# Rope's last two steps from GpSimd to VectorE, and the causal convolution's multiply-adds spread earlier, in a two-layer decoder trunk

## The chip, the core and the metric

The kernel runs on one core of a Trainium2 chip. A core has TensorE (matrix products and transposes, PE in the profile), VectorE (DVE), ScalarE (ACT), GpSimd (POOL) and SyncE (SP, which here only issues DMAs). The metric is the device time of one execution in microseconds; the kernel before takes 2527.41 us (median of three runs, 2525.86 to 2529.16).

## The reference, cut to what matters

Each of two layers does: a half-step SwiGLU feed-forward block, a mixer of three parallel branches, and another half-step feed-forward block. All data are float32, 512 positions by 1024 features. The change lies in the mixer:

```
qa, ka, va, qc, kc, vc, conv_in, gate_pre = split(h @ w_in)
rope(x)  = [x1*cos - x2*sin, x2*cos + x1*sin]        # on qa, ka, qc, kc; head size 64
oa = dilated_attention(rope(qa), rope(ka), va)       # 3 groups of 4 heads
z  = a * sigmoid(gt)                                 # a, gt = halves of conv_in, 512 channels
y[t] = sum_j w[j] * z[t - 30 + j] + b                # causal depthwise convolution, 31 taps
ob = silu(layernorm(y))                              # over the 512 channels
oc = differential_attention(rope(qc), rope(kc), vc)
x += postnorm((g0*proj_a(oa) + g1*proj_b(ob) + g2*proj_c(oc)) @ w_out)   # g = sigmoid gates
```

## The kernel before, in words

**Products.** Every float32 operand of a large product is split into a high part (`hi`, rounded by ScalarE, line 120) and a low part (`lo`, the difference, by VectorE, line 121); a product is then three matmuls (`mm3`, lines 138 to 140). `split` does this for a weight chunk of 128 columns. Four pairs of `hi` and `lo` buffers (`HLB`) let the splits run ahead of TensorE. The weights come through two 1 MB `raw` buffers, loaded by SyncE.

**Order of the work.** The program is one straight line; a planner places the instructions on each engine's queue by priority (earlier in the program first) among those that its own cost model takes to be ready. On the chip each queue is then worked off in that order, waits included.

**The mixer's order** (line 434 on): the first conv projection `conv(0)` (two of four channel tiles), eight differential q and k chunks with rope (`turned(0)`, `turned(1)`, which call `rotate`; `heads` after each), the differential value projection `vc`, the differential attention, twelve dilated q and k chunks with rope (`rope`; the first two of `qa` and of `ka` are plain, the other eight `phased`, written in strided order), the value projections `va0` and `va1`, the second conv projection `conv(2)`, dilated attention, and the gates and output projections (lines 760 to 809). Projections use three PSUM banks with the tag `pm`, and one `ps`.

**Rope** (`rotate`, lines 516 to 531). The projection lies in a PSUM bank. ScalarE copies it to `raw` (line 519), VectorE multiplies the bank by the cosine into the destination (line 526; the bank is free once both have read it), four DMAs issued by ScalarE's queue move the 32-row halves to `sw` (line 529), GpSimd multiplies `sw` by the sine (line 530) and adds it to the destination (line 531).

**The convolution.** The 31 taps of a channel tile are 31 VectorE instructions on `y` (lines 496 and 498), four tiles a layer, 124 in all. `conv_taps(rate)` puts the taps of the finished `z` tiles in a list, `tapq`, and sets `pace`; each later `split` takes up to `pace` taps off the list, and each tap gets an ordering edge behind that split's `lo`. In the kernel before, `conv_taps(2)` stands behind `vc` and the second `heads`, and `conv_taps(3)` behind the first dilated attention group. What is left at the end of the gates is put behind the last branch product (`flush`, lines 774 and 775). Then comes the convolution's layer norm: transposes of `y` (line 781), statistics, and transposes back (line 793).

Of the kernel before, what the change touches and what calls it, by code (L numbers as in the profile page):

```python
# [49 lines left out]
def kernel(ctx: ExitStack, tc: tile.TileContext, a, out):  # L50
    nc = tc.nc
    V, S, G, PE, SY = nc.vector, nc.scalar, nc.gpsimd, nc.tensor, nc.sync
# [10 lines left out]
    def bank(tag, shape=(P, T)):  # L63
        return psum.tile(list(shape), F32, tag=tag, name=tag, bufs=BANKS[tag])
# [47 lines left out]
    pace = [0]  # L112
# [18 lines left out]
    def col_chunks(src, c0, c1, step=256):  # L131
        for c in range(c0, c1, step):
            raw = load(src[:, c:c + step], KD, step)
            for s in range(0, step, P):
                yield c + s, split(raw[:, :, s:s + P])
# [6 lines left out]
    def proj_group(chunks, hh, hl):  # L142
        ps = [bank("pm") for _ in chunks]
        for p_, (wh, wl) in zip(ps, chunks):
            for k in range(KD):
                mm3(p_, wh[:, k, :], wl[:, k, :], hh[:, k, :], hl[:, k, :], k == 0, k == KD - 1)
        return ps
# [27 lines left out]
    def proj_lead(w, c0, c1, hh, hl, spare, raws=None):  # L175
        if raws is None:
            raws = [load(w[j][:, c:c + 256], KD, 256) for j, c in ((0, c0), (1, c1))]
        wts = {}
        for f in range(2):
            for j in range(2):  # L180
                raw = raws[j][:, :, f * P:(f + 1) * P]
                if (f, j) != (1, 1):
                    wh, wl = split(raw)
                    wts[f, j] = [(wh[:, k, :], wl[:, k, :]) for k in range(KD)]
                else:
                    wts[f, j] = []
                    for s in range(0, KD, 4):
                        pair_ = [z.rearrange("p (k n) -> p k n", n=P) for z in spare()]
                        wh, wl = split(raw[:, s:s + 4, :], pair_)
                        wts[f, j] += [(wh[:, k, :], wl[:, k, :]) for k in range(4)]  # L190
        H = T // 2
        whole = [bank("pm") for _ in range(2)]
        parts = []
        for s in range(2):
            c = slice(s * H, (s + 1) * H)
            two = bank(("pm", "po")[s])
            parts.append(two)
            outs = [whole[0][:, c], whole[1][:, c], two[:, 0:H], two[:, H:T]]
            for (f, j), o in zip(((0, 0), (0, 1), (1, 0), (1, 1)), outs):
                for k in range(KD):  # L200
                    wh, wl = wts[f, j][k]
                    mm3(o, wh, wl, hh[:, k, c], hl[:, k, c], k == 0, k == KD - 1, check=False)
        yield [(slice(0, T), whole[0], whole[1])]
        yield [(slice(s * H, (s + 1) * H), parts[s][:, 0:H], parts[s][:, H:T]) for s in range(2)]
# [229 lines left out]
    def mixer(l):  # L434
# [5 lines left out]
        def proj_t(chunk):  # L440
            return proj_group([chunk], hh, hl)[0]

        mrg = tc.tile_pool(name="mrg", bufs=1, side="right", reuse_waits="tile")
        with tc.tile_pool(name="mix", bufs=1, reuse_waits="tile") as mp:
# [10 lines left out]
            def ring(dt, name):  # L455
                return mp.tile([P, T], dt, tag="ring", name=name, bufs=20)

            def ztile(n, name):
                return mp.tile([P, n], F32, tag="zr", name=name, bufs=ZRB)
# [12 lines left out]
            with tc.tile_pool(name="att", bufs=1, reuse_waits="tile") as ap:  # L472
# [3 lines left out]
                def conv(c0):  # L476
                    cg0, ca0 = CV0 + 512 + c0 * P, CV0 + c0 * P
                    if c0 == 0:
                        zc = proj_lead((wi, wi), cg0, ca0, hh, hl, lambda: (ring(F32R, "wh"), ring(F32R, "wl")))
                    else:  # L480
                        zc = ([(slice(0, T), *proj_group([gc[1], uc[1]], hh, hl))]
                              for gc, uc in zip(col_chunks(wi, cg0, cg0 + 2 * P), col_chunks(wi, ca0, ca0 + 2 * P)))
                    for pieces in zc:
                        sg = sp.tile([P, T], F32, tag="t2k", name="sg", bufs=5)
                        z = cp.tile([P, CW - 1 + T], F32, tag="z", name="z", bufs=4)
                        V.memset(z[:, 0:CW - 1], 0.0)
                        zt = z[:, CW - 1:]
                        for c, pt, pz in pieces:
                            S.activation(sg[:, c], pt, AF.Sigmoid)
                            V.tensor_mul(zt[:, c], pz, sg[:, c])  # L490
                        taps.append(z)

                def tap(y, z, c, j, after):
                    with tc.issue_after(after.ins):
                        if j == 0:
                            V.tensor_scalar(y, z[:, 0:T], cw[:, c, 0:1], cb[:, c:c + 1], op0=ALU.mult, op1=ALU.add)
                        else:
                            V.scalar_tensor_tensor(y, z[:, j:j + T], cw[:, c, j:j + 1], y, op0=ALU.mult, op1=ALU.add)  # L498

                def conv_taps(rate):  # L500
                    pace[0] = rate
                    while taps:
                        z, c = taps.pop(0), len(ys)
                        y = cp.tile([P, T], F32, tag="y", name="y", bufs=4)
                        ys.append(y)
                        tapq.extend(lambda after, y=y, z=z, c=c, j=j: tap(y, z, c, j, after) for j in range(CW))

                conv(0)

                cs = ap.tile([P, CST_W - P], F32, tag="cs", name="cs")  # L510
                SY.dma_start(cs, a["cst"][:, P:])
                cos, sin = cs[:, 0:T], cs[:, T:2 * T]
# [3 lines left out]
                def rotate(ps, scale, d, phased):  # L516
                    raw = ztile(T, "raw")
                    sw = ztile(T, "sw")
                    S.activation(raw, ps, AF.Copy, scale=scale)
                    if phased:  # L520
                        dv = d.rearrange("p (r i) -> p i r", r=4)
                        vw = lambda z: z.rearrange("p (i r) -> p i r", r=4)
                    else:
                        dv = d
                        vw = lambda z: z
                    V.scalar_tensor_tensor(dv, vw(ps), scale, vw(cos), op0=ALU.mult, op1=ALU.mult)
                    for b in range(4):
                        s = (b ^ 1) * 32
                        S.dma_start(sw[b * 32:(b + 1) * 32], raw[s:s + 32])
                    G.tensor_mul(sw, sw, sin)  # L530
                    G.tensor_add(dv, dv, vw(sw))

                def rope(c0, n, scale, phased):
                    dst = []
                    ch = col_chunks(wi, c0, c0 + n * P)
                    for i in range(n):
                        d = ring(F32, "qk")
                        dst.append(d)
                        rotate(proj_t(next(ch)[1]), scale, d, phased(i))
                    return dst  # L540
# [35 lines left out]
                def proj_n(c0, n, stat, tag):  # L576
                    res = [ap.tile([P, n], F32, tag=tag, name="v", bufs=4) for _ in range(NT)]
                    kn = 4 if n == T else KD
                    ps = [bank(b_, (P, n)) for b_ in ("pm", "pm", "pm", "ps")]
                    for k0 in range(0, KD, kn):  # L580
                        raw = load(wi[k0 * P:(k0 + kn) * P, c0:c0 + n], kn, n)
                        for s in range(0, kn, kn // 2):
                            wh, wl = split(raw[:, s:s + kn // 2, :])
                            for u in range(kn // 2):
                                k = k0 + s + u
                                for t in range(NT):
                                    mm3(ps[t], stat(hh, k, t), stat(hl, k, t), wh[:, u, :], wl[:, u, :],
                                        k == 0, k == KD - 1)
                    for t in range(NT):
                        if t % 2:  # L590
                            V.tensor_copy(res[t], ps[t])
                        else:
                            S.activation(res[t], ps[t], AF.Copy)
                    return res
# [8 lines left out]
                d23 = turned(1)  # L603
                vc = proj_n(VC0, 512, nat, "vv")
                hc += heads(d23)
                conv_taps(2)

                def stile(n, name):
                    tag, bufs = ("t2k", 5) if name == "s" else ("h", 4)
# [44 lines left out]

                qa = rope(QA0, 6, -0.125, lambda i: i >= 2)
                ka = rope(KA0, 6, 1.0, lambda i: i >= 2)
                va0 = proj_n(VA0, 256, nat, "va0")

                oc_hl = [[ring(F32R, "oc") for s in "hl"] for h in range(4)]
# [244 lines left out]
```

## Time and profile before

| | |
|---|---|
| median of three runs | 2527.41 us |
| profiled execution, its own time | 2526.2 us |
| profiled execution, span from first to last instruction | 2524.4 us |
| mean granted TensorE clock | 0.993 |
| PE / DVE / ACT / POOL busy | 98% / 69% / 47% / 10% of the span |

A busy PE is one with a matmul in flight; the span less PE's busy time is 58.9 us. The mixers are two stretches of some 540 us, the first from about 372 us on and the second from about 1625 us on. All times of the trace are counted from the span's start.

### The profile page before, as it was taken

What the parts mean: (1) busy time and instruction counts of PE and PEld (TensorE: products, weight loads), DVE (VectorE), ACT (ScalarE), POOL (GpSimd) and SP (SyncE); (2) the same over time, 40 slices, a digit from 0 to 9 for tenths busy, and PEclk for the clock granted to TensorE, in tenths of its full rate; (3) what the DMA queues carried; (4) which work ended last, traced back from release to release, by engine and by line L of the source; (5) the groups of instructions that cost most, each with busy time, mean ns of one, the idle gap of its engine ahead of it and who ended that gap; (6) DMA issues with size and microseconds to landing.
All of it is one profiled execution on the core that took longest, in us unless ns stands there. A gap on an engine that the chain in (4) does not pass through costs nothing.

```text
span 2524.4 us, 36883 instructions
## 1 busy us (share of the span) xinstructions
PE 2465.5 (98%) x14956; PEld 2190.3 (87%) x14956; DVE 1735.6 (69%) x2354; ACT 1174.8 (47%) x1953; POOL 246.9 (10%) x156
## 2 busy tenths in 40 slices
PE   8999999999999999999989999999899999999999
PEld 8999888778787889998889998887787878899987
DVE  8777554796577487775497774546965764877753
ACT  5545444633523354445454454446235244544552
POOL 0000012060011110000000000130600111100000
PEclk9999999999999999999999999999999999999999
DMA  4333335242132423333233332451421224233322
GB/s 160 105 108 114 105 123 169 73 129 81 43 96 76 162 72 108 110 101 109 76 106 112 101 108 101 136 163 54 133 89 39 92 75 159 76 101 101 110 100 75
DMA packets 211850, 261.92 MB, mean 104 GB/s; under 512 B 8160, under 2 KB 167264, under 8 KB 211424
## 3 DMA queue, kind: packets, MB, share of 16 engines
q1 hardware_dynamic: 204000, 249.06, 30.1%
q10 hardware_dynamic: 7680, 10.50, 1.6%
q8 instruction: 118, 1.93, 0.3%
q14 instruction: 52, 0.43, 0.1%
HBM read 237.47 MB, written 6.29 MB: 97 GB/s over the span
## 4 chain that ended last, share of the span: by engine, by line
PE 88%; DVE 7%; ACT 2%; issue 2%; DMA 1%; SPq 0%; DVEq 0%; ACTq 0%
PE pm L138 11%; PE pm L139 11%; PE pm L140 11%; PE ps L308 6%; PE ps L314 6%; PE ps L313 6%; PE pm L313 2%; PE pm L308 2%; PE pm L314 2%; DVE y L498 2%; PE ps L139 2%; PE ps L140 2%; PE ps L138 2%; DVE lo L121 2%; PE pt L140 2%; PE pt L138 2%
## 5 line engine op out<-in xcount | busy, mean ns | idle before, releaser
L121 DVE TENSOR_TENSOR lo<-raw,hi 128x1024 fp32r<-128x1024 f32 x354 | 458.5, 1296 | 380.3 <-ACT hi L120 380.3
L120 ACT ACTIVATE hi<-raw 128x1024 fp32r<-128x1024 f32 x354 | 373.7, 1057 | 324.0 <-PE ps L139 127.2
L138 PE MATMUL pm<-hb,lo 128*128 128x512 f32 (+1 forms) x848 | 325.0, 383 | 0.0
L139 PE MATMUL pm<-hb,hi 128*128 128x512 f32 (+1 forms) x848 | 324.2, 382 | 0.0
L140 PE MATMUL pm<-hb,hi 128*128 128x512 f32 (+1 forms) x848 | 323.7, 382 | 0.0
L308 PE MATMUL ps<-t,lo 128*128 128x256 f32 x960 | 272.2, 284 | 4.3 <-ACT pm L381 4.3
L314 PE MATMUL ps<-t,hi 128*128 128x256 f32 x960 | 271.7, 283 | 0.0
L313 PE MATMUL ps<-t,hi 128*128 128x256 f32 x960 | 271.6, 283 | 0.0
L121 DVE TENSOR_TENSOR lo<-s,hi 128x1024 fp32r<-128x1024 f32 x160 | 194.9, 1220 | 69.1 <-ACT hi L120 68.9
L498 DVE SCALAR_TENSOR_TENSOR y<-z,ppl,y 128x512 f32<-128x512 f32 x240 | 214.4, 894 | 4.1
L120 ACT ACTIVATE hi<-s 128x1024 fp32r<-128x1024 f32 x160 | 164.8, 1052 | 88.4 <-DVE s L379 87.2
L308 PEld LDWEIGHTS ps<-t,lo 128*128 128x128 f32 x960 | 184.2, 192 | 5.3 <-ACT pm L381 5.3
L138 PEld LDWEIGHTS pm<-hb,lo 128*128 128x128 f32 x848 | 159.6, 188 | 31.9 <-issue 1.8
L139 PEld LDWEIGHTS pm<-hb,hi 128*128 128x128 f32 x848 | 159.5, 188 | 29.9 <-issue 0.7
L140 PEld LDWEIGHTS pm<-hb,hi 128*128 128x128 f32 x848 | 159.5, 188 | 29.9 <-issue 0.8
L314 PEld LDWEIGHTS ps<-t,hi 128*128 128x128 f32 x960 | 184.3, 192 | 0.0
L313 PEld LDWEIGHTS ps<-t,hi 128*128 128x128 f32 x960 | 184.3, 192 | 0.0
L240 POOL TENSOR_TENSOR h<-x,gain 128x512 f32<-128x512 f32 x40 | 54.0, 1370 | 1128.8 <-DVE x L299 1087.8
L120 ACT ACTIVATE ih<-inner 128x512 fp32r<-128x512 f32 x176 | 106.0, 622 | 82.6 <-PE ps L140 49.1
L121 DVE TENSOR_TENSOR il<-inner,ih 128x512 fp32r<-128x512 f32 x176 | 118.0, 687 | 38.3 <-ACT ih L120 38.3
L308 PE MATMUL pm<-hb,lo 128*128 128x256 f32 x480 | 135.8, 283 | 0.0
L313 PE MATMUL pm<-hb,hi 128*128 128x256 f32 x480 | 135.8, 283 | 0.0
(331 smaller groups left out, 6153.9 us busy)
## 6 DMA issues: line engine op xcount, KB each, us to landing
raw<-in_w_in_dram SPq DMA_DIRECT2D x62, 1024.0 KB, 5.4
raw<-in_ffn_w_gate_dram SPq DMA_DIRECT2D x43, 1024.0 KB, 5.0
raw<-in_ffn_w_up_dram SPq DMA_DIRECT2D x43, 1024.0 KB, 5.0
raw<-in_ffn_w_down_dram SPq DMA_DIRECT2D x40, 1024.0 KB, 4.9
sw<-raw ACTq DMA_DIRECT2D x160, 64.0 KB, 2.0
raw<-in_w_out_dram SPq DMA_DIRECT2D x8, 1024.0 KB, 4.9
raw<-in_ffn_w_down_dram SPq DMA_DIRECT2D x8, 512.0 KB, 3.4
xd<-x SPq DMA_DIRECT2D x16, 256.0 KB, 3.6
```

The source lines that it names most:

```text
L120: S.activation(hi, raw, AF.Copy)
L121: last = V.tensor_sub(lo, raw, bc(hi))
L138: PE.matmul(ps, sl, mh, start=first, stop=False, skip_group_check=not check)
L139: PE.matmul(ps, sh, mh, start=False, stop=False, skip_group_check=not check)
L140: PE.matmul(ps, sh, ml, start=False, stop=last, skip_group_check=not check)
L240: G.tensor_mul(h[j], xs[t][:, j * T:(j + 1) * T], g[:, j * T:(j + 1) * T])
L308: PE.matmul(dst[:, f, :], sl, m[:, 0, :], start=start and f == 0 and k == 0, stop=False, skip_group_check=True)
L313: PE.matmul(dst[:, f, :], sh, m[:, 0, :], start=False, stop=False, skip_group_check=True)
L314: PE.matmul(dst[:, f, :], sh, m[:, 1, :], start=False, stop=k == 3, skip_group_check=True)
L498: V.scalar_tensor_tensor(y, z[:, j:j + T], cw[:, c, j:j + 1], y, op0=ALU.mult, op1=ALU.add)
```

## The change

In `rotate` the sine product and the addition are issued to VectorE and no longer to GpSimd. The taps of the first two channel tiles begin right behind `conv(0)`, one behind each split; from the first dilated value projection (`va0`) on, three go behind each split. `conv_taps(3)` behind the first dilated attention group stays as it is.

```diff
                 conv(0)
+                conv_taps(1)
...
                     for b in range(4):
                         s = (b ^ 1) * 32
                         S.dma_start(sw[b * 32:(b + 1) * 32], raw[s:s + 32])
-                    G.tensor_mul(sw, sw, sin)
-                    G.tensor_add(dv, dv, vw(sw))
+                    V.tensor_mul(sw, sw, sin)
+                    V.tensor_add(dv, dv, vw(sw))
...
                 vc = proj_n(VC0, 512, nat, "vv")
                 hc += heads(d23)
-                conv_taps(2)
...
                 qa = rope(QA0, 6, -0.125, lambda i: i >= 2)
                 ka = rope(KA0, 6, 1.0, lambda i: i >= 2)
+                pace[0] = 3
                 va0 = proj_n(VA0, 256, nat, "va0")
```

## Rows read from the trace of the kernel before

**Rows 1.** The profile's page: busy us (share of the span) xinstructions, by engine.

```profile
PE 2465.5 (98%) x14956; PEld 2190.3 (87%) x14956; DVE 1735.6 (69%) x2354; ACT 1174.8 (47%) x1953; POOL 246.9 (10%) x156
```

**Rows 2.** Waits of PE, whole span: waiting line <- releaser: us in total, times, longest.

```profile
PE pm L138 <- DVE qk L526: 14.9, 4, 5.3
...
PE pt L793 <- DVE rstd L215: 7.0, 2, 3.5
...
PE pt L781 <- DVE y L498: 2.1, 2, 1.0
```

**Rows 3.** Windows, first mixer: start:end, us, busy by engine, granted clock, DMA.

```profile
560.00:570.00 10.00, 2.87 (x11) 2.58 (x12) 9.93 (x9) 1.47 (x2) 6.46 (x4) 0.62 0.46 138
...
790.00:812.00 22.00, 17.47 (x84) 13.71 (x83) 17.43 (x29) 12.61 (x17) 1.74 (x1) 0.92 0.22 73
```

**Rows 4.** Timeline of DVE, rope stage: start, us, engine, line, operation, tiles, xcount.

```profile
511.01 1.12 DVE L526 SCALAR_TENSOR_TENSOR qk<-pm,cs 128x512 f32<-128x512 f32 x1 [0.27 <-ACT raw L519]
...
547.29 0.68 DVE L526 SCALAR_TENSOR_TENSOR qk<-pm,cs 128x512 f32<-128x512 f32 x1
...
553.34 1.22 DVE L121 TENSOR_TENSOR lo<-raw,hi 128x1024 fp32r<-128x1024 f32 x1
...
560.24 3.67 DVE L498 SCALAR_TENSOR_TENSOR y<-z,ppl,y 128x512 f32<-128x512 f32 x2
...
568.54 1.03 DVE L526 SCALAR_TENSOR_TENSOR qk<-pm,cs 128x512 f32<-128x512 f32 x1
```

**Rows 5.** Timeline of POOL in the same stage.

```profile
559.31 2.38 POOL L531 TENSOR_TENSOR qk<-qk,sw 128x512 f32<-128x512 f32 x1
```

**Rows 6.** Line 498 alone, all 240 taps: ns min/median/max, first and last start.

```profile
L498 DVE SCALAR_TENSOR_TENSOR y<-z,ppl,y x240: 714/752/2048, 449.9 to 2054.2; 128x512 f32<-128x512 f32 x120
```

**Rows 7.** Timeline of PE, `va0`: first, after the long wait, full clock again, last.

```profile
559.16 0.28 PE L138 MATMUL pm<-hi,hb 128*128 128x256 f32 x1
...
564.90 0.58 PE L138 MATMUL pm<-hi,hb 128*128 128x256 f32 x1 [5.23 <-DVE qk L526]
...
572.72 0.27 PE L138 MATMUL pm<-hi,hb 128*128 128x256 f32 x1
...
580.86 0.29 PE L140 MATMUL ps<-lo,hb 128*128 128x256 f32 x1
```

**Rows 8.** Groups of DVE by line and shape: busy us, mean ns | idle before.

```profile
L121 DVE TENSOR_TENSOR il<-inner,ih 128x512 fp32r<-128x512 f32 x176 | 118.0, 687 | 38.3 <-ACT ih L120 38.3
...
L665 DVE TENSOR_SCALAR ocn<-ocn,rstd 128x128 f32<-128x128 f32 x32 | 11.8, 412 | 0.1
...
L465 DVE TENSOR_TENSOR oa<-pt,oa 128x512 fp32r<-128x512 f32 x4 | 4.1, 1065 | 0.7 <-ACT oa L464 0.7
```

**Rows 9.** Timeline of ACT, rope stage: two bank copies, one chunk's four DMA issues.

```profile
510.38 0.60 ACT L519 ACTIVATE raw<-pm 128x512 f32<-128x512 f32 x1 [1.66 <-PE pm L140]
...
511.01 2.44 ACTq L529 DMA_DIRECT2D sw<-raw  x4
515.82 0.60 ACT L519 ACTIVATE raw<-pm 128x512 f32<-128x512 f32 x1 [3.89 <-PE pm L140]
```

**Rows 10.** Line 529, all 160 DMAs: time from issue to landing.

```profile
DMA to landing us min/median/max: 1.9/2.0/6.6
```

**Rows 11.** Timelines of PE and DVE, end of the gates and the layer norm.

```profile
803.43 1.15 PE L781 MATMUL pt<-ident,y 128*128 128x128 f32 x8
808.07 3.89 PE L793 MATMUL pt<-ident,yn 128*128 128x128 f32 x16 [3.48 <-DVE rstd L215]
...
793.53 5.46 DVE L498 SCALAR_TENSOR_TENSOR y<-z,ppl,y 128x512 f32<-128x512 f32 x7
...
811.59 0.69 DVE L465 TENSOR_TENSOR ob<-y,ob 128x512 fp32r<-128x512 f32 x1 [2.75 <-ACT ob L464]
```

**Rows 12.** Timeline of ACT, differential attention: first and last DMA issue of one chunk.

```profile
488.29 0.52 ACTq L529 DMA_DIRECT2D sw<-raw  x1
...
503.43 0.60 ACTq L529 DMA_DIRECT2D sw<-raw  x1
```

## The prediction

> **What bounds the kernel now.** I read the busy shares first: TensorE (PE) is busy 98% of the span, VectorE (DVE) 69%, GpSimd (POOL) 10% [rows 1]. So only PE's idle time, 58.9 us (2524.4 less 2465.5), and its time at a low clock can be won, and the next view is who PE waits for. Three entries belong to code that the change touches: the rope's cosine product on line 526, 14.9 us in four waits; the layer norm's reciprocal on line 215, 7.0 us; the last convolution tap on line 498, 2.1 us [rows 2]. Then the windows show where: at 560 to 570 PE is busy 2.87 of 10 us while DVE is busy 9.93, and at 790 to 812 PE is busy 17.47 of 22 [rows 3]. The second mixer repeats both; every count in rows 2 is even.
>
> **Place one, the value projection `va0` behind the twelve rope chunks.** The bank copies of two rope chunks start 5.44 us apart, PE's pace [rows 9]. DVE starts its cosine products at 511.01 and, nine chunks later, at 568.54: 6.39 us a chunk [rows 4]. It falls behind 0.95 us a chunk, some 8.6 us in all, and holds the PSUM banks that `va0` needs. The reason is in the durations: a tap has a median of 752 ns but up to 2048 [rows 6], and two of them take 3.67 us [rows 4] beside a POOL addition that takes 2.38 [rows 5]. Each engine waits out the other's instruction.
>
> `va0` has 96 matmuls (8 k, 4 row tiles, 3 each). From 572.72 to 580.86 there are 68 intervals in 8.14 us, 0.12 each, so 95 intervals want 11.4 us; the first and the last start 21.7 apart [rows 7]. The place costs 10.3 us a layer. Of that some 7.5 are the two waits [rows 2], the rest the clock: 0.62 in that window [rows 3], between the levels of 1.2 and 2.4 GHz, behind a wait of 5.23 us [rows 7].
>
> **Place two, the convolution's layer norm.** Idle are 22 less 17.47, 4.5 us [rows 3]. Sixteen transposes take 3.89 us at the low clock where eight took 1.15 before the 3.48 us wait; that loses 3.89 less 2.30, 1.6 [rows 11]. So 6.1 us a layer. It starts late because the last seven taps run until 793.53 + 5.46 = 799.0 [rows 11].
>
> **The change, part by part.**
>
> *Taps.* Splits behind `conv(0)`: 4 + 4 of `turned`, 4 of `vc`, 12 of rope, one tap each, 24; then 2 of `va0`, 4 of `va1`, 4 of `conv(2)`, three each, 30. That is 54 of 62; 8 + 62 = 70 remain for the 24 splits of the gates, which take 72. Before: 22 splits at two, 44; 18 + 62 = 80 for 72 places, so 8 behind the last product. The 124 instructions stay 124; one tap less follows each rope split, and none is left at the end.
>
> *Sine product and addition.* 20 chunks a layer lose two POOL instructions and give VectorE two. The product is contiguous, two SBUF inputs, 128x512: 0.69, as line 121's group of that shape [rows 8]. A plain addition is the same. For a phased one, strided in one input and in the output, VectorE has no row of this form: from below 0.69; from above 1.48, if the 0.40 that a phased cosine product costs over a plain one (1.08, mean of 1.12 and 1.03, against 0.68 [rows 4]) is paid for the read and again for the write. I take 1.07, from line 465, which also reads and writes with a stride [rows 8].
>
> Per phased rope chunk DVE then has 1.08 + 1.22 (`lo` alone [rows 4]) + 0.75 (one tap) + 0.69 + 1.07 = 4.81; per plain chunk 0.68 + 1.22 + 0.75 + 0.69 + 0.69 = 4.03. The nine chunks counted above are seven phased and two plain, 41.7, plus 16 short line 665 instructions at 0.41 at most [rows 8], 6.6: 48.3 of PE's 49.0 us. It fits, barely, and the 0.41 holds POOL's share. With 1.48 it is 51.2, late by 2.2.
>
> *The added wait.* The product waits on VectorE's queue for four DMAs; behind it stand the addition, the next `lo`, a tap and the next cosine product. Issue takes 2.44 us [rows 9] and landing 2.0 [rows 10], so it can start 2.44 + 2.0 = 4.4 us after the bank copy, where the cosine product has ended at 1.1 and `lo` at 2.3. Up to 2 us of idle DVE a chunk, but no growing debt: the landing is set by ScalarE's queue, so a VectorE that is late finds its data landed. Costs nothing in the stage, since `lo` runs four buffers ahead.
>
> *What is late next at `va0`.* The last rope chunk's bank: PE ends about 559.3, the copy takes 0.60 [rows 9], the cosine product 1.08, the two handovers 0.27 each, as the idle time in front of one cosine product [rows 4]: 561.5. `va0` can meanwhile do some 12 matmuls in the other three banks, 1.4 us from 559.16 on [rows 7], to 560.6. That leaves 0.9, plus a VectorE late by, I take, 1.5 (one product and addition ahead of it): 2.4 us, a gain of 10.3 less 2.4 = 7.9 a layer (bounds 4 and 10.3).
>
> *Differential chunks.* There DVE gets 4.03 plus a head's difference of 0.69, 4.7 of 5.44 us; PE has no wait there now. A late cosine product at the end of that stage could hold `vc`: three of four banks give 9 matmuls, 2 us, before it is needed, against 2.1 late (product, addition, tap). I take a loss of 0.5 a layer (0 to 4).
>
> *Layer norm.* `y` is complete before PE leaves the branch products at about 790.4. From the last transposes of `y` (799.05) to the first `ob` difference (811.59) is 12.5 us; begun at 790.4 it ends at 803, while PE has two gate chunks of 5.44 and transposes, to about 804. So 6.1 goes but for about a microsecond: 5.0 (bounds: 1.0, the wait on `y` alone [rows 2], if the transposes of the second half stay behind the second gate chunk; and 6.1).
>
> **Sum.** 7.9 - 0.5 + 5.0 = 12.4 us a layer, 24.8 in two. The profiled execution took 2526.2, so 2501.4; the median shown is 1.2 higher: 2503.
>
> **A rule for and a rule against.** The trace shows two engines stretching each other, 0.75 to 2.05 us [rows 6]. The Trainium skill, "SBUF — State Buffer", section "SBUF: two separate sides", calls the shared port pair a lock held for a whole instruction while the loser "fully blocks"; the trace agrees: two taps beside a 2.38 us addition take 3.67 us in place of 1.50 [rows 4, 5]. Against the change stands the Trainium skill, "Perfetto Trace Analysis", section "Optimizing Scalar/DVE Operations": a saturated DVE should shed work, even to GpSimd, though the same paragraph doubts it for these two because they share a port. VectorE is saturated here (9.93 of 10 [rows 3]); by the rule's first half the time is that of rival D, and rows 6 speak for its second half.
>
> **Rivals.** A measurement of this kernel tells some 0.2%, 5 us, from no change.
>
> A, the layer norm keeps its order on PE and wins only the wait on `y`: 1.0 in place of 5.0, 2511. For it: PE's second eight transposes now stand behind the second gate chunk [rows 11]. Against: the first half's banks come free earlier. 14%.
>
> B, VectorE stays the bound of the rope stage, since the budget is 48.3 to 51.2 of 49.0 and the DMA waits take the rest: `va0` still waits some 6 us and the layer norm wins 3, (4.3 - 0.5 + 3.0) x 2 = 13.6, about 2514; with only 1.0 at the norm 2518. 9%.
>
> C, slower: in the differential attention the four DMAs of one chunk go out between 488.29 and 503.43 [rows 12], behind exponentials on ScalarE's queue. If the planner puts the product early, VectorE holds the softmax behind it until 503.43 + 2.0 = 505.5, up to 17.2 us a layer: 34.4 against 24.8, 2537. It decides from 12.4 us a layer on. Against: the planner knows ScalarE's order, so the product should stand behind the fourth DMA. 6%.
>
> D, slower, the stretched durations are VectorE's own and not due to GpSimd: then nine chunks of 6.39 gain 0.69 + 0.98 and lose one tap, 0.75: 0.92 each, 8.3 a layer later at `va0`, against 5.0 won: 3.3 a layer, 6.6 in all, 2534. Against: the median tap of 752 ns [rows 6]. 4%.
>
> E, the change of order gives back elsewhere what it wins (three taps a split in the value projections, `vc` held 4 us): within 0.2%. 5%.
>
> **How the numbers follow.** The forecast has 62%, by itself 2495 to 2509 (all recovered: 2 x 16.4 = 32.8, so 2494.6; or 4.0 at `va0`, 5.0 at the norm, nothing lost: 2509). To hold 8 in 10 the range takes in A and the better half of B: 2493 to 2518. Faster: 62 + 14 + 9 = 85%; same 6%; slower 9%, as C and D can end in between.
>
> **What would show it.** Right: no wait of `va0` on line 526 over 2.5 us; taps of 0.75 in the rope stage, additions near 1.07 when phased, 0.69 when plain; lines 530 and 531 gone from POOL; nothing behind the last branch product; no 3.5 us wait at line 793. Wrong: cosine products still 6 us apart; a softmax waiting behind a product on `sw`; additions over 1.5 us; PE waiting at `vc`.

## The result, and the profile after

The changed kernel takes 2501.86 us (median of 4 runs, 2499.92 to 2505.38), the kernel before beside it 2528.28 (4 runs, 2525.86 to 2532.91): a ratio of 0.9895, 95% interval 0.9881 to 0.9909. The profiled execution took 2499.98 us, its span is 2498.2. The forecast was 2503 us, with a range of 2493 to 2518.

The page of the changed kernel, busy us by engine:

```profile
PE 2460.8 (99%) x14956; PEld 2187.9 (88%) x14956; DVE 1731.3 (69%) x2434; ACT 1174.0 (47%) x1951; POOL 110.9 (4%) x76
```

GpSimd lost 80 instructions and VectorE gained 80, yet VectorE is busy 4.3 us less than in [rows 1]. The new ones cost it 27.4 us (products) and 34.0 (additions); its other instructions became shorter by more than that (a stretched instruction counts as busy for its whole length), the taps alone by 31.9 us, from 214.4 (mean 894 ns) to 182.5. VectorE's tap group in the changed kernel (busy us, mean ns | idle before), and line 498 by itself, which answers to [rows 6]:

```profile
L498 DVE SCALAR_TENSOR_TENSOR y<-z,ppl,y 128x512 f32<-128x512 f32 x240 | 182.5, 760 | 3.6
```

```profile
L498 DVE SCALAR_TENSOR_TENSOR y<-z,ppl,y x240: 731/749/1778, 392.2 to 2008.2; 128x512 f32<-128x512 f32 x120
```

PE's waits after (waiting line <- releaser: us in total, times, longest). In the changed kernel the cosine product is line 527, the sine product 531, the addition 532, the two transposes of the norm 782 and 794:

```profile
PE pm L138 <- DVE qk L527: 2.6, 2, 1.5
```

The 14.9 us of [rows 2] are 2.6, and both entries of the layer norm are gone. The same two windows as [rows 3], after:

```profile
560.00:570.00 10.00, 8.88 (x74) 8.68 (x74) 9.89 (x12) 1.66 (x2) 0.00 (x0) 1.00 0.44 132
790.00:812.00 22.00, 21.74 (x103) 17.39 (x103) 12.49 (x14) 15.09 (x21) 2.99 (x2) 1.00 0.23 73
```

VectorE is as full as before in the first (9.89 of 10), with 12 instructions in place of 9; PE has its 8.88 and the whole clock. One chunk of VectorE's timeline, which answers to [rows 4]:

```profile
555.06 1.08 DVE L527 SCALAR_TENSOR_TENSOR qk<-pm,cs 128x512 f32<-128x512 f32 x1
555.96 0.69 DVE L531 TENSOR_TENSOR sw<-sw,cs 128x512 f32<-128x512 f32 x1
556.56 1.22 DVE L121 TENSOR_TENSOR lo<-raw,hi 128x1024 fp32r<-128x1024 f32 x1
557.69 1.10 DVE L532 TENSOR_TENSOR qk<-qk,sw 128x512 f32<-128x512 f32 x1
558.68 0.76 DVE L498 SCALAR_TENSOR_TENSOR y<-z,ppl,y 128x512 f32<-128x512 f32 x1
559.34 0.55 DVE L496 TENSOR_SCALAR y<-z,ppl 128x512 f32<-128x512 f32 x1
559.93 0.75 DVE L498 SCALAR_TENSOR_TENSOR y<-z,ppl,y 128x512 f32<-128x512 f32 x1
560.60 1.03 DVE L527 SCALAR_TENSOR_TENSOR qk<-pm,cs 128x512 f32<-128x512 f32 x1
```

Cosine products start 5.54 us apart, here and on the average of the nine chunks of [rows 4], and the last one starts at 560.60 instead of 568.54. PE at `va0`, first the last matmul before its wait, then the wait, against 5.23 in [rows 7]:

```profile
560.29 0.28 PE L138 MATMUL pm<-hi,hb 128*128 128x256 f32 x1
561.68 0.39 PE L138 MATMUL pm<-hi,hb 128*128 128x256 f32 x1 [1.12 <-DVE qk L527]
```

Lines 531 and 532 by themselves (ns min/median/max): nothing stretches them, and VectorE's wait for the four DMAs, which I had feared for the whole stage, comes four times:

```profile
L531 DVE TENSOR_TENSOR sw<-sw,cs x40: 674/683/697, 406.8 to 1810.0; 128x512 f32<-128x512 f32 x40
...
  DMA sw<-raw: 5.8, 4
```

```profile
L532 DVE TENSOR_TENSOR qk<-qk,sw x24: 672/1080/1135, 508.9 to 1811.9; 128x512 f32<-128x512 f32 x24
L532 DVE TENSOR_TENSOR d<-d,sw x16: 683/686/693, 408.5 to 1688.3; 128x512 f32<-128x512 f32 x16
```

The layer norm, which answers to [rows 11]: transposes of `y` on PE, the last tap of the layer and the first statistics on VectorE. The last tap ends 34 us earlier than before (765.4 against 799.0), and what follows waits for nothing:

```profile
781.13 1.04 PE L782 MATMUL pt<-ident,y 128*128 128x128 f32 x8
...
786.11 0.60 PE L782 MATMUL pt<-ident,y 128*128 128x128 f32 x4
...
764.62 0.75 DVE L498 SCALAR_TENSOR_TENSOR y<-z,ppl,y 128x512 f32<-128x512 f32 x1
...
781.93 1.29 DVE L785 BATCH_NORM_STATS2 bs<-pt 128x6 f32<-128x512 f32 x2
```

**Where the 26 us came from.** I cut each mixer by starts in the trace. Stage A runs from the first matmul of `conv(0)` that reads `wl` and writes the bank `po` to the first transposes of `ocn` behind `va0` (392.0 to 581.0 in the first layer before); stage B from there to the last matmul on `ob` (866.0). In us, first / second layer; time and ratio to the kernel before, measured beside it, with its 95% interval:

| kernel | stage A | stage B | median, us | ratio |
|---|---|---|---|---|
| before | 189.0 / 189.2 | 285.0 / 285.1 | 2528 to 2530 | 1 |
| after | 180.1 / 180.4 | 279.0 / 278.9 | 2501.86 | 0.9895 (0.9881, 0.9909) |
| e1 engine only | 181.1 / 180.9 | 285.3 / 285.4 | 2513.6 | 0.9945 (0.9928, 0.9962) |
| e2 taps only | 187.8 / 185.1 | 279.1 / 280.3 | 2507.72 | 0.9921 (0.9905, 0.9937) |
| e3 two taps to the end | 179.5 / 179.2 | 286.1 / 285.1 | 2508.74 | 0.9921 (0.9906, 0.9936) |
| e4 idle GpSimd product | 188.7 / 191.1 | 278.9 / 279.0 | 2517.85 | 0.9958 (0.9943, 0.9973) |
| e7 sine product on GpSimd | 185.5 / 188.3 | 278.9 / 278.9 | 2509.74 | 0.9921 (0.9908, 0.9935) |
| e8 GpSimd memset | 180.0 / 180.6 | 279.0 / 278.9 | 2502.2 | 0.989 (0.9875, 0.9904) |
| e11 change again | 180.3 / 180.7 | 280.3 / 278.9 | 2500.01 | 0.9887 (0.987, 0.9903) |
| e12 pre-norm fused, again | 179.9 / 180.4 | 278.9 / 279.0 | 2492.04 | 0.9851 (0.9835, 0.9866) |

The change won 8.9 and 8.8 us in A, 6.0 and 6.2 in B: 29.9. The span shrank by 26.2, so some 4 were given back outside both stages (below).

### The profile page after: what moved, and what is told of

It reads as the page before. It is cut to its first block, busy times and chain, and to the rows that moved or that the text cites. A ratio compares the mean times of both kernels' runs of the same rounds, so it can differ in the third digit from the quotient of the medians.

```text
span 2498.2 us, 36829 instructions
## 1 busy us (share of the span) xinstructions
PE 2460.8 (99%) x14956; PEld 2187.9 (88%) x14956; DVE 1731.3 (69%) x2434; ACT 1174.0 (47%) x1951; POOL 110.9 (4%) x76
## 4 chain that ended last, share of the span: by engine, by line
PE 92%; DVE 3%; ACT 2%; DMA 1%; issue 1%; SPq 0%; ACTq 0%; DVEq 0%
PE pm L138 12%; PE pm L139 12%; PE pm L140 12%; PE ps L308 6%; PE ps L314 6%; PE ps L313 6%; PE pm L313 2%; PE pm L308 2%; PE pm L314 2%; PE ps L140 2%; PE ps L139 2%; PE ps L138 2%; PE pt L140 2%; PE pt L139 2%; PE pt L138 2%; PE pt L314 1%
## 5 line engine op out<-in xcount | busy, mean ns | idle before, releaser
L121 DVE TENSOR_TENSOR lo<-raw,hi 128x1024 fp32r<-128x1024 f32 x354 | 444.3, 1255 | 374.3 <-ACT hi L120 374.0
L498 DVE SCALAR_TENSOR_TENSOR y<-z,ppl,y 128x512 f32<-128x512 f32 x240 | 182.5, 760 | 3.6
L313 PE MATMUL pm<-hb,hi 128*128 128x256 f32 x480 | 135.8, 283 | 0.0
L314 PE MATMUL pm<-hb,hi 128*128 128x256 f32 x480 | 135.8, 283 | 0.0
```

Source lines behind the costliest of these rows:

```text
L121: last = V.tensor_sub(lo, raw, bc(hi))
L313: PE.matmul(dst[:, f, :], sh, m[:, 0, :], start=False, stop=False, skip_group_check=True)
L314: PE.matmul(dst[:, f, :], sh, m[:, 1, :], start=False, stop=k == 3, skip_group_check=True)
```

## The experiments

**Which part wins what.** e1 has the kernel before with only the two instructions moved; e2 has the changed kernel with only these two back on GpSimd.

```diff
 e1 (against before)                     e2 (against after)
-G.tensor_mul(sw, sw, sin)              -V.tensor_mul(sw, sw, sin)
-G.tensor_add(dv, dv, vw(sw))           -V.tensor_add(dv, dv, vw(sw))
+V.tensor_mul(sw, sw, sin)              +G.tensor_mul(sw, sw, sin)
+V.tensor_add(dv, dv, vw(sw))           +G.tensor_add(dv, dv, vw(sw))
```

> The sine product and addition on VectorE, taps as in the kernel before (two behind each rope split, eight left for the end of the gates). Theory (two separate gains: at va0 from the lock between GpSimd and VectorE, at the layer norm from the left-over taps): the rope chunk costs VectorE one tap more than with the whole change, 5.56 us phased and 4.78 plain, nine chunks about 52 of PE's 49 us, so va0 waits again, some 3 to 4 us a layer, and the layer norm gains nothing: about 6 us won a layer, 2513 to 2518, with taps at 0.75 us in the rope stage. Rival (the engine alone pays for all): within 4 us of the whole change, 2498 to 2506.

> The taps as changed, the sine product and addition on GpSimd as before. Theory: the lock stays, some 2.3 us a rope chunk beside 4.1 of work that had two taps; with one tap the chunk takes VectorE about 5.6 of PE's 5.44 us, so most of the debt at va0 goes all the same (7 to 9 us a layer won of 10.3) and the layer norm's 6 are won in full: 2500 to 2507, with taps still stretched to 2 us. Rival (without the move of the two instructions VectorE stays the bound of the rope stage): va0 keeps its wait of 5 us and its low clock, only the layer norm is won: 2513 to 2518.

PE's waits in e1, then in e2:

```profile
PE pt L793 <- DVE rstd L215: 7.0, 2, 3.5
...
PE pm L138 <- DVE qk L526: 4.0, 2, 2.0
...
PE pt L781 <- DVE y L498: 2.1, 2, 1.1
```

```profile
PE pm L138 <- DVE qk L527: 10.0, 3, 5.8
```

The move alone wins 7.9 and 8.3 us in A and nothing in B; the taps alone win 5.9 and 4.8 in B, and 1.2 and 4.1 in A, less than I had expected. So the taps are place two. By stages the parts sum to 31.6 us, the whole to 29.9: they share place one, of which there were only 10.3 us a layer to win. How they share it is not shown. e2's profiled execution is its slowest (2515.19, clock 0.992), and the other five take 2504.79 to 2508.14 (clock 0.994 to 0.997); in which stage those win their 7 us or more no profile tells. By the ratios the taps alone win some 20 us and the move alone some 14, of the 26 that both win together. So either alone takes a part of place one, and that the move takes the larger part holds for this one profile. e2's median is 0.7 us above the range that I gave, and one of its waits at `va0`, 5.8 us, is the one that its rival named.

**Does the price of place two lie in the last taps?** e3 lets two taps, not three, follow each split of the value projections and `conv(2)`, so that taps are left behind the last branch product.

```diff
-                pace[0] = 3
+                pace[0] = 2
```

> The whole change, but two taps and not three behind each split from va0 on: 10 taps fewer before the gates, so eight are left for the end as in the kernel before. Theory: the layer norm waits again for y, loses its 6.1 us a layer and keeps the rest: 2510 to 2515, PE waits on line 215's reciprocal or on the last tap about 4.5 us a layer. Rival (the layer norm gains because VectorE is free of the rope's debt, not because of the taps): within 3 us of the whole change, 2499 to 2505.

```profile
PE pt L794 <- DVE rstd L215: 7.0, 2, 3.5
...
PE pt L782 <- DVE y L498: 2.1, 2, 1.0
```

The waits of [rows 2] are back to the digit, and B is as long as before. The median was 1.3 us below the range I gave; the stages are as expected.

**Is it the lock, and what takes it?** e4 adds to each rope chunk a GpSimd product whose result nobody reads, e8 a GpSimd memset of the same buffer, and e7 puts the sine product alone back on GpSimd.

```diff
 e4
+                    G.tensor_mul(raw, raw, sin)
 e8
+                    G.memset(raw, 0.0)
 e7
-                    V.tensor_mul(sw, sw, sin)
+                    G.tensor_mul(sw, sw, sin)
```

> The whole change, and in each rope one more product on GpSimd, of raw by the sine, written over raw, which nothing reads afterwards; it leaves the outputs as they are. Theory (the lock): each product of 1.3 us holds VectorE up by about as much, 6.1 us a rope chunk against PE's 5.44, so va0 waits some 4 to 6 us a layer, with a low clock behind it: 2508 to 2522, and VectorE's two-input instructions beside it take 1.3 us longer. Rival (the long durations were VectorE's own queue, not GpSimd): within 3 us of the whole change, 2499 to 2505, taps at 0.75.

> The whole change, and in each rope a memset of raw on GpSimd at the place where the run with the extra GpSimd product had that product; nothing reads raw afterwards, the outputs stay as they are. Theory (what holds VectorE up is a GpSimd instruction that reads SBUF while VectorE has two SBUF inputs, as the Trainium skill, SBUF - State Buffer, section SBUF: two separate sides, says): a memset reads nothing, so VectorE's durations stay (lo 1.22, taps 0.75) and the time is that of the whole change, 2499 to 2506. Rival (any GpSimd instruction holds it up): as with the extra product, 2513 to 2520.

> The change with the sine product back on GpSimd; the addition stays on VectorE and the taps go as after the change. Theory (GpSimd reading SBUF holds VectorE, and the price goes by GpSimd instructions a chunk): one such instruction a chunk as in e4_pool_product, whose stage A was 188.7 and 191.1 us, but VectorE also loses one product of 0.69 us a chunk: the cosine products 5.6 to 5.9 us apart, stage A 181 to 187 us, the wait of va0 3 to 7 us in the two layers, time 2504 to 2513. Rival one (VectorE's own load alone counts): VectorE has less to do than after the change, so stage A is 180 or less and the time 2498 to 2502. Rival two (the added handover between two engines costs by itself): the addition waits on VectorE's queue for GpSimd's product, stage A over 188 us and time over 2514.

e4: one `lo` on VectorE beside the added product, one without, and the product:

```profile
517.32 1.22 DVE L121 TENSOR_TENSOR lo<-raw,hi 128x1024 fp32r<-128x1024 f32 x1
...
520.72 2.28 DVE L121 TENSOR_TENSOR lo<-raw,hi 128x1024 fp32r<-128x1024 f32 x1
```

```profile
520.37 1.55 POOL L531 TENSOR_TENSOR raw<-raw,cs 128x512 f32<-128x512 f32 x1 [3.98 <-DMA sw<-raw]
```

The second `lo` ends at 523.0, 1.08 after the product's end at 521.92: it has waited for the end of an instruction with which it shares no data, and then taken about its usual time. e4 loses 16.0 us against the change, and A is as long as before it. e8's memsets lengthen nothing. Of the `lo`, taps and sine products that ran beside one, none took over 1.24, 0.75 and 0.69 us. A memset is shorter than e4's product (0.53 against 1.3 us), but a hold of that length would show:

```profile
L531 POOL MEMSET raw<- x40: 524/526/661, 406.3 to 1805.7; 128x512 f32 x40
```

```profile
L532 DVE TENSOR_TENSOR sw<-sw,cs x40: 676/685/705, 408.2 to 1808.8; 128x512 f32<-128x512 f32 x40
```

The Trainium skill, "SBUF — State Buffer", section "Who interferes with whom", says that VectorE with two SBUF inputs contends with a GpSimd instruction that reads SBUF and not with one that only writes it; e4 (2517.85) and e8 (2502.2) agree on both halves.

e7's time came out in the upper half of the theory's range. Stage A did so in the first layer; in the second it is 188.3, above that range and where rival two had it. Half the GpSimd work costs more than half of A's win, 5.4 of 8.9 us and 7.9 of 8.8. Beside the hold there is a second price: VectorE waits for GpSimd's product in its own queue (first fence), and PE waits at `vc`, which it does in neither kernel (second fence):

```profile
  POOL sw L531: 17.2, 8
```

```profile
PE pm L138 <- DVE qk L527: 7.1, 2, 3.8
...
PE pm L138 <- DVE d L527: 3.6, 2, 2.2
```

How the loss divides between the two prices is not shown.

**The GpSimd work that is left.** After the change GpSimd still runs the pre-norm's first product and the gate sums. e5 folds the former into VectorE's second product; e6 moves the latter to VectorE; e11 and e12 repeat after and e5 on one chip.

```diff
 e5, e12
-                if not first:
-                    G.tensor_mul(h[j], xs[t][:, j * T:(j + 1) * T], g[:, j * T:(j + 1) * T])
...
-                    V.tensor_scalar_mul(h[j], h[j], r)
+                V.scalar_tensor_tensor(h[j], xs[t][:, c], r, g[:, c], op0=ALU.mult, op1=ALU.mult)
 e6
-                    G.tensor_add(m_, gts[0][j], gts[1][j])
+                    V.tensor_add(m_, gts[0][j], gts[1][j])
...
-                    G.tensor_add(gts[j], gts[j], ms[dp + j])
+                    V.tensor_add(gts[j], gts[j], ms[dp + j])
```

> The whole change, and the five prenorms that multiply by the gain on GpSimd (1.37 us each, 40 in all) do it in one VectorE instruction with the scale, 0.75 in place of 0.54 us. Theory (work on GpSimd costs only where VectorE's queue holds PE back): at the prenorms PE waits 2.3 us each for h, which comes after ScalarE's sum of squares and reciprocal, so little changes: 2498 to 2504, PE's waits on h within 2 us of 7.6 in all. Rival (every GpSimd product beside VectorE costs PE its 1.3 us): 5 us or more faster than the whole change, below 2497.

> The whole change, and the 32 sums of the gated branches on VectorE in place of GpSimd, so GpSimd has only the prenorms left. Theory: in the gates VectorE is not the bound (39 of 50 us) and PE waits 1.0 us in all, so nothing is to be had: 2499 to 2505. Rival (the lock costs wherever it is met): 3 us or more faster, below 2498.

> The changed kernel, unaltered, beside the other three on the same chip: 2498 to 2506 us; 24 to 29 us below the kernel before. If the low clock behind the 2.3 us wait at the feed-forward entries comes and goes by itself, its profile shows it at another set of the four entries than the first profile (0.83 to 0.86 at 903 to 914, 1255 to 1275 and 2148 to 2158 us); if it belongs to this order of instructions, at the same three.

> The kernel of e5_prenorm_on_vector, unaltered, beside the changed kernel on the same chip. If the fused pre-norm product is worth what the first run showed: 2492 to 2498 us, 4 to 8 us below e11_change_again. If that was a difference between chips: within 2 us of e11_change_again.

e6: 2503.12 us (2498.62 to 2506.03), ratio 0.9888 (0.9873, 0.9903): no change, as expected; PE doesn't wait there. e5: 2495.87 (2493.01 to 2496.6), ratio 0.9863 (0.985, 0.9876), below the 2498 to 2504 that I expected and in the range that I had given its rival, and e12, 2492.04 (2490.75 to 2492.63), lies 8.0 us below e11 (2499.31 to 2502.91) with no overlap. It is the fastest kernel here. PE's waits in e11 that are changed or gone in e12, then what e12 has in their place:

```profile
PE pt L252 <- DVE h L247: 8.0, 3, 7.4
PE pt L252 <- DVE h L249: 7.6, 5, 2.5
...
PE pm L138 <- DVE wl L121: 2.9, 2, 1.8
...
PE pm L171 <- DVE hb L255: 1.5, 1, 1.5
```

```profile
PE pt L247 <- DVE h L244: 17.8, 8, 7.3
```

Those four make 20.0; 17.8 are left, so the waits explain 2.2 of the 8.0, and the 1.3 us for every GpSimd product, which the rival had as the cause, is not shown. Of the rest, a lower granted clock can explain up to some 5: four windows of 10 us have a granted clock of 0.83 in e11 (at 80, 660, 1250 and 1260), one in e12 (at 1250), and 10 us at 0.83 lose 1.7. That part is a reckoning from two profiles, not shown by an experiment.

**Two taps at `va0` only.** e9 and e10 set `pace` to 2 ahead of `va0` and to 3 ahead of `va1`, e10 with e5's edit.

```diff
-                pace[0] = 3
+                pace[0] = 2
                 va0 = proj_n(VA0, 256, nat, "va0")
+                pace[0] = 3
```

> The whole change, but two taps behind each of the two va0 splits and three from va1 on: 52 taps before the gates and 72 for their 72 places, so none is left over. Theory: with two a split VectorE's cosine product at the end of the rope stage comes sooner (the run with two throughout waited 0.3 us a layer there in place of 1.1 and 1.5) and the layer norm keeps its gain: 1 us a layer faster than the whole change, 2497 to 2502. Rival (the last tap, now behind the last split, comes too late for the layer norm): 2505 to 2512.

> The pre-norm's first product fused into VectorE's second, as in e5_prenorm_on_vector, and two taps a split in va0, three from va1 on, as in e9_two_at_va0. Theory (each wins what it won in the undisturbed layers: some 6 us from the pre-norm, 0.5 us a layer at va0): 2493 to 2498, waits of PE on the cosine product under 2 us in all. Rival (the order of the dilated attention in the first layer that goes with two taps draws a granted clock near 0.5 for some 40 us while PE is busy): then the first layer's window 640 to 680 us shows it again and the time is 2507 to 2514.

e9 took 2517.03 us (6 runs, 2497.53 to 2520.34), ratio 0.993 (0.9904, 0.9956), a miss of my range and of the rival's. Its stages are as expected, 179.7 us in A twice and 278.9 in the second B; the loss is in the first layer's dilated attention, at a granted clock of a half and with PE never idle:

```profile
640.00:645.00 5.00, 5.00 (x27) 3.85 (x26) 1.73 (x7) 2.00 (x7) 0.00 (x0) 0.68 0.06 20
645.00:675.00 30.00, 30.00 (x125) 23.77 (x124) 6.93 (x30) 11.72 (x38) 0.00 (x0) 0.50 0.01 2
675.00:680.00 5.00, 5.00 (x22) 4.39 (x22) 1.87 (x10) 1.19 (x5) 0.00 (x0) 0.57 0.00 2
```

e10 took 2492.56 us (6 runs), ratio 0.9874 (0.9848, 0.99): four runs lie between 2491.99 and 2492.76, the other two at 2508.08 and 2509.65, about 16 us above. Its profile is of a run at 2492 and has full clock there. So the low clock comes in some executions and not in others, also in e9, where one run took 2497.53; e11 has it for a shorter time at the same place (0.83 at 660 to 670, PE busy 10.00 of 10). What draws it stays open. Beside e12, two taps win nothing.

## Why the prediction was right

**Place one: 7.9 a layer forecast, 8.9 and 8.8 measured.** The mechanism is as told: taps and `lo` without GpSimd beside them keep their own length, VectorE falls from 6.39 to 5.54 us a chunk against PE's 5.44, and `va0` finds its banks. The budget was 48.3 us for nine chunks, and the additions took 1.08 (1.07 taken). The term mis-sized is the residual wait, 2.4 us: 0.9 for the last bank's chain and 1.5 for a VectorE that comes late behind a product and an addition. PE waits 1.12 (1.5 in the second layer). The bank's copy ends at 559.65 and the cosine product starts at 560.60; with the handover of 0.27 VectorE was 0.7 late, behind one tap, since that chunk's product and addition stand behind its cosine product and not in front of it. With two taps a split in place of three there, the two waits fall from 2.6 us to 1.4 (e9). The clock stays full through this wait (1.00 in the window above).

**The added wait** costs what was forecast, nothing: VectorE is idle 5.8 us before line 531 in the whole span. The loss of 0.5 at `vc` didn't come either, and PE has no wait there; e7 shows that the danger was real (3.6 us in two waits).

**Place two: 5.0 a layer forecast, 6.0 and 6.2 measured,** of the 6.1 to be had. The start is as told: the norm begins where PE leaves the branch products, at 781.13, which is the 790.4 of the forecast less the 9 us won ahead of it. The term mis-sized is the microsecond kept back. From there to the first `ob` difference at 795.19 it takes 14.1 us and not 12.5 (the 799.05 from which I counted are the last two of the first eight transposes of `y`; the last eight stand at 803.43 [rows 11]). But PE fills all of it with its gate chunks and transposes, and the first `ob` matmul starts at 795.9. The taps are done with room to spare: I counted 72 places for 70 taps as if splits kept pace with PE. They run up to four buffers ahead of it, so the last tap ends at 765.4, 16 us before PE reaches the transposes of `y`. With eight taps left over the price is back, whatever engine has the rope (e1 and e3); with none left it is gone even with rope's last two steps on GpSimd (e2).

**What I didn't foresee: some 4 us given back.** After a wait of 2.5 us or less of PE on the pre-norm's `h`, at the entries of the feed-forward blocks, the granted clock falls in some executions. Windows of after at three such places:

```profile
900.00:914.00 14.00, 11.70 (x87) 11.52 (x86) 14.00 (x18) 4.58 (x9) 3.51 (x2) 0.88 0.22 76
1255.00:1275.00 20.00, 16.57 (x119) 16.22 (x118) 19.23 (x26) 7.69 (x13) 2.54 (x2) 0.83 0.45 152
...
2150.00:2160.00 10.00, 10.00 (x73) 10.00 (x73) 9.47 (x11) 4.66 (x6) 0.00 (x0) 0.84 0.01 2
```

and the same three in e11, the same kernel:

```profile
900.00:914.00 14.00, 11.69 (x99) 11.44 (x98) 13.46 (x20) 5.65 (x14) 3.52 (x2) 1.00 0.24 76
1255.00:1275.00 20.00, 16.05 (x108) 15.70 (x109) 17.68 (x28) 7.17 (x19) 4.45 (x3) 0.83 0.48 159
...
2150.00:2160.00 10.00, 8.62 (x73) 8.65 (x74) 10.00 (x12) 3.66 (x5) 0.00 (x0) 1.00 0.01 2
```

In the first these cost up to 14 x 0.12 + 20 x 0.17 + 10 x 0.16 = 6.7 us (PE is idle for a part of them); the kernel before lost up to 20 x 0.09 = 1.8 in its like window (0.91 at 1630 to 1650), where after has 1.00. That is about 5 for the some 4 given back. The kernel before has the same three waits, of 2.3, 2.5 and 2.3 us, and the full clock behind each (1.00 at 921 to 935, 1275 to 1295 and 2177 to 2190), so the wait alone does not bring it. Two of the three places differ between executions of one kernel. At 1255 the clock is low in both: there the two can't tell chance from the order of the instructions. The two errors, 5 us too little won and 4 given back, hid each other; the forecast of 2503 is better than its terms.

**The rivals.** A (the norm keeps its order on PE): no, the second eight transposes of `y` start at 786.11, before the second gate chunk, and nothing in the norm waits. B (VectorE still the bound): it is at 9.89 of 10, but the pace suffices; e7 is where it would have gone. C (the softmax held up by the DMAs): no, VectorE waits 5.8 us for them in all. D (durations VectorE's own): excluded by e1 and e4. E (the order gives back all): some 4 of 30.

The Trainium skill, "Perfetto Trace Analysis", section "Optimizing Scalar/DVE Operations", which says that taking some work off a saturated VectorE, even to GpSimd, "may make sense" and so spoke for D, is not borne out here: VectorE was at 9.93 of 10 [rows 3], and taking two more instructions a chunk won 8 us a layer (e1). The doubt in the same paragraph is.

## What to carry to other kernels

Before handing elementwise work to GpSimd, compare the median with the maximum of VectorE's instructions beside it: 752 against 2048 ns [rows 6] gave the hold away, and a full VectorE became faster with more to do. An instruction that sits in the gap between two engines costs twice, by its stay and by its handover (e7). Work deferred to "behind every split" ends where the splits end, not where the products do, so count its places by the producer's lead.

## What the runs showed of the hardware

- A strided float32 operand cost the same here whether an instruction had one (the phased cosine product writes with a stride: median 1080 ns) or two (the phased addition reads and writes with one: 1080); plain ones take 692 and 686. My upper bound of 1.48 us, the stride paid twice, was wrong.
- A GpSimd instruction of 526 ns that only writes SBUF left VectorE's two-input instructions at their length (e8: 685 ns); one of 1.55 us that reads it goes with a `lo` of 2.28 us in place of 1.22 (e4).
- The cosine product, with one of its inputs in PSUM, was not stretched: in the kernel before it took at most 1155 ns, also beside GpSimd's instructions, and 1115 after, where taps went up to 2048 and 1778.
- The granted clock can fall to 0.50 for 30 us while PE shows no idle time at all (e9, 645 to 675 us: 125 matmuls in 30 us; after has full clock from 640 to 680). It costs that execution about 16 us.
